# A fused two-block transformer step: TensorE products ordered by tiling, output projections with PSUM tiles taken one by one, and at most four weight pieces waiting for their split

## The chip, the cores and the metric

One NeuronCore of a Trainium2 chip runs the whole program in one launch. The metric is the device time of one execution in microseconds. In the profile PE is TensorE, PEld its weight loads, DVE VectorE, ACT ScalarE, POOL GpSimd and SP SyncE, which issues nearly all DMAs.

## The reference

256 tokens of width 1024 pass through two blocks. All inputs and outputs are float32.

```python
# first block
h = rms_norm(x, norm_mix_g)
(f_q, f_k, f_v, f_f, n_q, k_c, v_c, k_s, v_s, k_w, v_w, n_g, g_a, g_b) = split_cols(h @ w_in)
out_a = fox_attention(...) @ w_fox_up          # 8 heads of 64, with forget gates
out_b = nsa_attention(...) @ w_nsa_up          # compressed, selected and window branches
x = x + (sigmoid(g_a) * out_a + sigmoid(g_b) * out_b) @ w_out
x = x + hierarchical_moe(rms_norm(x, norm_ffn_g), ...)   # 16 experts, 2 per token, SwiGLU of width 512
# second block, two layers
h = rms_norm(x, g_pre)
q_h, f_h, i_h, z_h, q_a, k_a, v_a, z_a = split(h @ w_in)
o_h = rms_norm(hgrn2(q_h, f_h, i_h, lb), g_head) * silu(z_h)     # 8 heads of 128
o_a = sliding_window_attention(rotary(q_a), rotary(k_a), v_a, sinks) * silu(z_a)   # 16 heads of 64
x = x + rms_norm(concat(o_h, o_a) @ w_out, g_post)
```

## The kernel before

**Stages.** The program runs layer 1 of the first block (`layer1`), the experts (`moe`), and two hybrid layers (`hybrid`). Its stages lie in the trace at about 0 to 250 us, 250 to 490 us, 500 to 748 us and 748 to 1003 us. Between two stages an `Edge` adds the result to x, normalises it and transposes it for the next projection.

**A planner writes the order.** The code does not issue instructions directly. Each piece of work is a generator, a task, which yields operations; `Sched.run` (L331) keeps a modelled clock for every engine, and picks for each engine the next operation of all tasks by a key: operations that cannot start within 40 ns of the engine's clock come after those that can, then the smaller priority number goes first, then the older task. Priorities (L409) are P_EDGE -1, P_SPLIT 0, P_EVAC 1, P_SIDE 2, P_LATE 3, P_MAIN 9. The order so found is fixed in each engine's queue when the program is built; on the chip an instruction that isn't ready holds up those behind it on its engine. Waits of a task for another (`wait`, `Flag`) are waits in the planner only: they shape the order. All operations are issued on one line, L216, so the trace tells them apart by tile names. Where the model finds TensorE idle, `keep_warm` (L790) fills in products of a tile of ones (`warm<-ones`).

**Products.** The big projections split both operands into two float32r parts and do three products for each float32 one (`mm3`, `mm3_col`); these use the whole 128 by 128 array. Their outputs go to four PSUM tiles (`acc`); everything else shares four more (`bank`). Other products are plain float32, which the trace shows as two records each. Some use half of the array: 64 output columns (`128*64`: the experts, `bank<-ha` in the scores of hgrn2, `bank<-ap,kv` in the attention's second product), or 64 rows (`64*128`: `bank<-kv,qaT`, the attention's first product), or both. Transposes are products with an identity (`bank<-cp,...`).

**Weights.** `loader` (L512) loads pieces of 1 MB in a fixed plan into 23 shared slots of 1 MB, while fewer than `K.raw_max` are loaded and unused (3 in most of the program, up to 19 in the experts). A piece of a projection is then split: ScalarE writes the high part (`w<-raw`), VectorE the low one (`w<-raw,w`), in two halves, while fewer than `K.half_max` halves are in use. The experts' pieces are used as they are (`"whole"`, `"pair"`). Splits have P_SPLIT, those of output projections P_LATE.

**The experts** (L1342 on). Each expert e takes up to 64 tokens. The main task does gate and up, gu(e): 16 float32 products of 512 columns in pairs that write the two halves of the PSUM partitions (32 records `bank<-raw,xt`); then down(e - 1) (16 records `bank<-raw,route`). Beside them run `rows_of(e)` (L1460: the one-hot rows of the expert by two transposes, and four small products; it writes `ws`, the weights that hidden(e) scales with), `hidden(e)` (L1529: the SwiGLU, then two transposes to hT for down(e)), and `combine(e)` (L1546: down(e)'s result is scaled and added to four `acc` tiles by four products `acc<-rows`). For every four experts `group` gathers tokens by products of x, split by `halves` (L1477) into `xh` and `xl` once.

**The output projection** (`out_proj`, L678) takes all four `acc` tiles first:

```python
    ps = []
    for i in range(4):
        p = yield from acc_tile(K, [128, 512])
        ps.append(p)
```

In a hybrid layer there are four groups of inputs. Groups 0 and 1 are the hgrn2 heads 0 to 3 and 4 to 7, and the main task waits for a group's heads before it goes on to it; groups 2 and 3 are the attention. The last projection is z3: `c_z` (L1802) reads its `acc` tile in four steps on ScalarE and VectorE and only then releases it, and `heads(3)` (L1888) goes on from there to `og`, which group 1 reads.

## Time and profile before

| what | us |
|---|---|
| median of 3 runs (lowest, highest) | 1006.81 (1002.85, 1007.44) |
| the profiled execution | 1005.22 |
| its span, first to last instruction | 1003.4 |
| PE busy in the span | 975.9 |
| DVE busy | 701.4 |
| ACT busy | 496.7 |

A row of the timeline gives start, busy time, engine, line, operation, the tiles out<-in, rows*columns of the array and the moving operand's size, and how many like records follow each other; a bracket gives idle time before it and who ended it. Matmuls are pipelined, and their ends are modelled, so the time that a product takes of the engine is read from start to next start. A PE that is shown as busy may be filling in ones.

### The profile page before, as it was taken

How to read it: one execution, taken by the hardware profiler on the slowest of the kernel's cores; microseconds unless marked ns; L12 is line 12 of the kernel's file. 1: busy time of each engine (PE TensorE's matmuls, PEld its weight loads, DVE VectorE, ACT ScalarE, POOL GpSimd, SP SyncE). 2: the span in 40 equal slices, each digit the busy share in tenths (PEclk: the TensorE clock that was granted, in tenths of full speed). 3: DMA queues.
4: the chain of work that ended last, by engine and by line, in shares of the span. 5: the costliest groups of instructions: out<-in, count | busy, mean ns of one | idle time of the engine just before them, and what ended most of it. 6: DMA issues, size and time to landing. Idle time of an engine off the chain costs nothing.

```text
span 1003.4 us, 16635 instructions
## 1 busy us (share of the span) xinstructions
PE 975.9 (97%) x6335; PEld 748.5 (75%) x6335; DVE 701.4 (70%) x1755; ACT 496.7 (50%) x1054; POOL 23.2 (2%) x64
## 2 busy tenths in 40 slices
PE   7999999999999999999899999999999999999998
PEld 6877898897434343434588979888888897988887
DVE  5777888685364444545656898999768489899942
ACT  5556679741121111114335658668664365866841
POOL 0101000000000000000000000000000000000000
PEclk9999999999999999999999999999999999999999
DMA  8822593797899999989910224433936232442321
GB/s 299 293 81 85 170 318 113 266 378 269 302 390 388 407 409 409 409 343 391 363 63 1 84 84 128 130 104 120 336 122 218 67 103 86 130 146 102 125 107 42
DMA packets 106578, 210.33 MB, mean 210 GB/s; under 512 B 6174, under 2 KB 54544, under 8 KB 106496
## 3 DMA queue, kind: packets, MB, share of 16 engines
q1 hardware_dynamic: 105248, 206.00, 57.3%
q0 software_dynamic: 1248, 3.22, 1.0%
q8 instruction: 52, 0.85, 0.4%
q14 instruction: 30, 0.25, 0.1%
HBM read 208.16 MB, written 1.05 MB: 208 GB/s over the span
## 4 chain that ended last, share of the span: by engine, by line
PE 46%; DVE 8%; ACT 1%; issue 1%; DVEq 0%
PE acc L216 32%; PE bank L216 12%; DVE ha L216 3%; DVE w L216 2%; PE warm L216 1%; DVE ap L216 1%; ACT ha L216 1%; DVE hb L216 1%; DVE hn L216 0%; DVE rows L216 0%; DVE tiny L216 0%; DVE x L216 0%; DVE og L216 0%; DVE za L216 0%; ACT w L216 0%
## 5 line engine op out<-in xcount | busy, mean ns | idle before, releaser
L216 DVE TENSOR_TENSOR w<-raw,w 128x1024 fp32r<-128x1024 f32 (+1 forms) x196 | 233.2, 1211 | 28.5 <-ACT w L216 27.4
L216 PE MATMUL acc<-hh,w 128*128 128x256 f32 x1280 | 247.4, 289 | 0.0
L216 ACT ACTIVATE w<-raw 128x1024 fp32r<-128x1024 f32 (+1 forms) x196 | 198.7, 1040 | 46.7 <-PE acc L216 26.4
L216 PEld LDWEIGHTS acc<-hh,w 128*128 128x128 f32 x1280 | 202.9, 192 | 6.2 <-issue 4.1
L216 PE MATMUL acc<-hl,w 128*128 128x256 f32 x640 | 184.8, 289 | 0.0
L216 PE MATMUL acc<-w,hh 128*128 128x512 f32 (+2 forms) x512 | 155.5, 380 | 0.2
L216 PEld LDWEIGHTS acc<-hl,w 128*128 128x128 f32 x640 | 122.6, 192 | 2.3 <-issue 0.7
L216 PE MATMUL bank<-raw,xt 128*64 128x512 f32 x512 | 118.1, 599 | 1.2 <-DVE xt L216 1.2
L216 PEld LDWEIGHTS acc<-w,hh 128*128 128x128 f32 x512 | 92.6, 188 | 17.3 <-issue 2.2
L216 PE MATMUL acc<-w,hl 128*128 128x512 f32 (+2 forms) x256 | 96.6, 377 | 0.0
L216 PE MATMUL acc<-w,og 128*128 128x512 f32 x384 | 88.7, 390 | 0.0
L216 PEld LDWEIGHTS acc<-w,og 128*128 128x128 f32 x384 | 71.9, 188 | 14.8
L216 ACT ACTIVATE route<-bank,route 128x256 f32<-128x256 f32 x16 | 7.6, 473 | 144.9 <-PE bank L216 144.9
L216 PEld LDWEIGHTS bank<-raw,xt 128*64 128x64 f32 x512 | 33.6, 136 | 58.5 <-issue 53.0
L216 DVE TENSOR_TENSOR ha<-ha 128x128 f32<-128x128 f32 (+5 forms) x216 | 69.3, 352 | 0.6
L216 ACT ACTIVATE ap<-ap,tiny 128x256 f32<-128x256 f32 (+1 forms) x98 | 42.9, 448 | 49.0 <-DVE tiny L216 36.5
L216 PE MATMUL bank<-raw,route 128*64 128x512 f32 x256 | 60.3, 604 | 0.0
L216 PEld LDWEIGHTS acc<-w,hl 128*128 128x128 f32 x256 | 48.3, 189 | 8.2 <-issue 1.0
L216 PE MATMUL warm<-ones 128*128 128x256 f32 x275 | 40.1, 297 | 4.6 <-ACT ones L437 2.4
L216 PEld LDWEIGHTS warm<-ones 128*128 128x128 f32 x275 | 36.3, 198 | 8.1 <-ACT ones L437 2.4
L216 PEld LDWEIGHTS bank<-raw,route 128*64 128x64 f32 x256 | 17.4, 138 | 31.8 <-issue 29.5
L216 PE MATMUL bank<-ha 128*64 128x96 f32 (+2 forms) x608 | 37.9, 246 | 0.0
(276 smaller groups left out, 1330.3 us busy)
## 6 DMA issues: line engine op xcount, KB each, us to landing
raw<-in_w_in_dram SPq DMA_DIRECT2D x68, 1024.0 KB, 7.5
raw<-in_w_gate_dram SPq DMA_DIRECT2D x64, 512.0 KB, 8.9
raw<-in_w_up_dram SPq DMA_DIRECT2D x64, 512.0 KB, 9.9
raw<-in_w_down_dram SPq DMA_DIRECT2D x32, 1024.0 KB, 11.5
raw<-in_w_out_dram SPq DMA_DIRECT2D x20, 1024.0 KB, 5.2
raw<-in_cmp_k_w_dram SPq DMA_DIRECT2D x2, 1024.0 KB, 5.7
raw<-in_cmp_v_w_dram SPq DMA_DIRECT2D x2, 1024.0 KB, 5.8
raw<-in_w_fox_up_dram SPq DMA_DIRECT2D x2, 1024.0 KB, 12.2
```

The lines of the kernel that those rows point to most:

```text
L216: go = lambda: f(*a, **k)
```

## The change

The planner now knows tilings. An operation on TensorE has a mode: whether its rows and its columns are at most 64, for plain float32 products; all others count as whole. Its model adds 95 ns (`SWITCH`) to a product of another mode than the last, and 2 ns in place of 53 for the second of two products side by side. In the choice of the next product, one of a task between P_EDGE and P_MAIN whose mode is not the current one goes behind the main task until 1.5 us (`GATHER`) after it was ready.

In the experts, a flag for each one, `gate[e]`, is set when gu(e) has been issued. `rows_of(e)` does its mask on VectorE as before and then waits for `gate[e]`; the transposes of `hidden(e)` wait for `gate[e + 1]`; the four products of `combine(e)` wait for `gate[e + 2]`. `hidden` and `combine` of the last two experts have P_EDGE. `halves` does its work in 8 pieces of 256 columns in place of 2 of 1024.

`out_proj` takes each of its four PSUM tiles when its first product comes. The loader counts, in `K.parts`, loaded pieces that are to be split, and loads a further one only while there are fewer than four.

```diff
--- before.py
+++ after.py
@@ -82,11 +82,12 @@
 
 class Op:
 
-    __slots__ = ("alts", "ins", "outs", "half", "ready", "banks", "rows")
+    __slots__ = ("alts", "ins", "outs", "half", "ready", "banks", "rows", "mode")
 
     def __init__(self, alts, ins, outs, half=(0, 2)):
         self.alts, self.ins, self.outs, self.half, self.ready = alts, ins, outs, half, None
         self.banks = ()
+        self.mode = None
 
 
 class _Eng:
@@ -140,6 +141,7 @@
         self.cols = [0.0, 0.0]
         self.readers = {}
         self.work, self.cold = [], True
+        self.mode, self.turned = (False, False), False
         self.fill = self.halfway = None
         self.slot = {}
         self.acc = {}
@@ -220,6 +222,7 @@
             half = (h, h + 1)
         o = Op([(eng, op, cost, go)], reg(ins), reg(outs), half)
         if eng == "PE":
+            o.mode = (ins[0].shape[0] <= 64, aps[0].shape[0] <= 64) if op == "matmul" and ins[-1].dtype == F32 else (False, False)
             o.rows = ins[0].shape[0] / 128 * min(1.0, n / 0.6 / cost if op == "matmul" and ins[-1].dtype == F32 else 1.0)
         else:
             o.banks = {self.slot.get(x.tensor.name, x.tensor.name) for x in aps if str(x.space) == "PSUM"}
@@ -271,6 +274,11 @@
     def _product(self, o, start, cost):
         lo, hi = o.half
         start = max(start, self.clk["PE"])
+        if o.mode != self.mode:
+            self.mode = o.mode
+            start += SWITCH
+            self.clk["PE"] = start
+            self.cols = [max(c, start) for c in self.cols]
 
         self.cold = self.activity(start) < (WARM[1] if self.cold else WARM[0])
         if self.cold:
@@ -278,7 +286,7 @@
 
         other = max(o.ready, self.cols[lo]) + cost
         beside = hi - lo == 1 and other <= self.clk["PE"] + 100
-        end = max(start + 53, other) if beside else start + cost
+        end = max(start + 2, other) if beside else start + cost
         if not beside:
             self.work.append((start, end, o.rows))
         for h in range(lo, hi):
@@ -360,7 +368,11 @@
                                     if e != eng:
                                         r = max(r, end + self.LAT[e])
                             late = r > c + (HOLD if t.prio == P_EDGE else 40)
-                            key = (late, r if late else 0.0, -1 if t is self.halfway and eng == "PE" else t.prio, t.seq)
+                            prio = -1 if t is self.halfway and eng == "PE" else t.prio
+
+                            if eng == "PE" and t.pend.mode != self.mode and P_EDGE < t.prio < P_MAIN and r < t.pend.ready + GATHER:
+                                prio = P_MAIN + 0.1
+                            key = (late, r if late else 0.0, prio, t.seq)
                             if pick is None or key < pick[0]:
                                 pick = (key, r, t, alt)
                 if pick is not None and (best is None or pick[1] < best[1]):
@@ -410,6 +422,7 @@
 
 WINDOW, WARM, FILL = 3413.0, (0.43, 0.7), (350.0, 0.7)
 TO_PE, IDLE = 200.0, 150.0
+SWITCH, GATHER = 95.0, 1500.0
 HOLD = 200
 SLOTS = 23
 TINY = 11
@@ -438,6 +451,7 @@
     K.plan, K.next, K.hold = [], 0, 0
     K.accs, K.banks = Res(4), Res(4)
     K.slots, K.tinies = Res(SLOTS), Res(TINY)
+    K.parts = 0
     K.raws, K.raw_max, K.halves, K.half_max = 0, 3, 0, 4
     K.eps = K.const.tile([128, 1], F32, name="eps")
     nc.vector.memset(K.eps, EPS)
@@ -486,6 +500,9 @@
     done = False
 
 
+WHOLE = ("whole", "pair")
+
+
 class Unit:
     def __init__(self, key, pieces, a, n, how):
         self.key, self.pieces, self.a, self.n, self.how = key, pieces, a, n, how
@@ -518,8 +535,10 @@
     def load():
         yield ("if", lambda: K.go)
         for i, u in enumerate(K.plan):
-            yield ("if", lambda: K.raws < K.raw_max and K.slots.free)
+            whole_ = u.how in WHOLE
+            yield ("if", lambda: K.raws < K.raw_max and K.slots.free and (whole_ or K.parts < 4))
             K.raws += 1
+            K.parts += not whole_
             raw, s = yield from big(K, [128, 2048], "raw")
             rv = raw[:, :u.a * u.n].rearrange("p (a n) -> p a n", a=u.a)
             for src, c in u.pieces:
@@ -540,12 +559,13 @@
         u.flag[j].done = True
         if all(f.done for f in u.flag):
             K.raws -= 1
+            K.parts -= 1
             K.slots.release(raws.pop(i)[1])
 
     sch.spawn(load(), P_SPLIT)
     for i, u in enumerate(K.plan):
         yield wait(loaded[i])
-        if u.how in ("whole", "pair"):
+        if u.how in WHOLE:
             u.half = raws.pop(i)
             u.flag[0].done = True
             continue
@@ -679,14 +699,13 @@
 
 
 
-    ps = []
-    for i in range(4):
-        p = yield from acc_tile(K, [128, 512])
-        ps.append(p)
+    ps = {}
     n = len(groups)
     us = {}
 
     def go(g, c, j, t):
+        if 2 * t + c not in ps:
+            ps[2 * t + c] = yield from acc_tile(K, [128, 512])
         oh, ol = groups[g][1]()
         wh, wl = yield from half(K, us[g][c], j)
         for a in range(2):
@@ -1446,6 +1465,8 @@
     t_w = [sp(weights(t), P_EVAC) for t in range(2)]
     groups = {}
 
+    gate = [Flag() for _ in range(NE)]
+
     class Group:
         pass
 
@@ -1459,10 +1480,11 @@
 
     def rows_of(e):
 
-        yield wait(t_w, t_rows.get(e - 1), ys.get(e - 2))
+        yield wait(t_w, t_rows.get(e - 1))
         for t in range(2):
             yield nc.vector.tensor_scalar(dup[:, t].rearrange("p (i s) -> p i s", i=2),
                                           K.c("slot")[:, None, :].to_broadcast([128, 2, CAP]), posm[:, t, e:e + 1], None, op0=OP.is_equal)
+        yield wait(gate[e] if e else None, ys.get(e - 2))
         p2, b_ = yield from bank(K, [128, 258])
         for t in range(2):
             yield nc.tensor.transpose(p2[:, t * 128:(t + 1) * 128], dup[:, t], ident)
@@ -1479,7 +1501,9 @@
         for nm in ("xh", "xl"):
             xhl.append((yield from big(K, [128, 2, D], nm, F32R)))
         for t in range(2):
-            yield from split(K, *(a[0][:, t].rearrange("p (k d) -> p k d", k=8) for a in xhl), K.x[:, t].rearrange("p (d k) -> p k d", k=8))
+            for k in range(0, 8, 2):
+                yield from split(K, *(a[0][:, t].rearrange("p (k d) -> p k d", k=8)[:, k:k + 2] for a in xhl),
+                                 K.x[:, t].rearrange("p (d k) -> p k d", k=8)[:, k:k + 2])
 
     def both(a, b):
         yield wait(a)
@@ -1534,6 +1558,7 @@
         yield nc.vector.scalar_tensor_tensor(s, pg[:, 0], r, s, op0=OP.mult, op1=OP.mult)
         yield nc.vector.scalar_tensor_tensor(s, pg[:, 1], r, s, op0=OP.mult, op1=OP.mult)
         K.banks.release(b_)
+        yield wait(gate[e + 1] if e < NE - 1 else None)
         ph, b_ = yield from bank(K, [128, 2, 128])
         for b in range(2):
             yield nc.tensor.transpose(ph[:, b], s[:, 128 * b:128 * b + 128], ident)
@@ -1552,8 +1577,9 @@
             w = ws[r, 0, e:e + 1]
             yield scaled(K, ty[r, c], py[r], w)
             yield nc.vector.scalar_tensor_tensor(ty[o, c], py[r], w, ty[r, c].bitcast(F32), op0=OP.mult, op1=OP.subtract)
-        yield wait([sp(part(c), P_EVAC if e < NE - 1 else P_EDGE) for c in range(2)])
+        yield wait([sp(part(c), P_EVAC if e < NE - 2 else P_EDGE) for c in range(2)])
         K.banks.release(b_)
+        yield wait(gate[e + 2] if e < NE - 2 else None)
         for t in range(2):
             for c in range(2):
                 yield nc.tensor.matmul(acc[2 * t + c][0], P2[:, e % 2, t], ty[:, c], start=(e == 0), stop=(e == NE - 1))
@@ -1573,7 +1599,7 @@
                     yield nc.tensor.matmul(py[64 * c:64 * c + 64], hT[:, e % 2, b, 64 * h:64 * h + 64], w[:, b, 512 * c:512 * c + 512],
                                            start=(h + b == 0), stop=(h + b == 2))
             drop_whole(K, u)
-        ys[e] = sp(combine(e, py, b_), P_EVAC if e < NE - 1 else P_EDGE)
+        ys[e] = sp(combine(e, py, b_), P_EVAC if e < NE - 2 else P_EDGE)
 
     def bounds():
         K.raw_max -= 1
@@ -1604,11 +1630,12 @@
                     c = w.rearrange("p i (b f) -> p i b f", b=2)[:, :, a, 256 * h:256 * h + 256]
                     yield nc.tensor.matmul(pg[64 * h:64 * h + 64], g.xt[:, k, j], c, start=(k == 0), stop=(k == 7))
             drop_whole(K, u)
+        gate[e].done = True
         if j == 3:
             K.slots.release(g.s_x)
             if q < 3:
                 sp(group(q + 1), P_EVAC)
-        hid[e] = sp(hidden(e, pg, b_), P_EVAC)
+        hid[e] = sp(hidden(e, pg, b_), P_EVAC if e < NE - 2 else P_EDGE)
         if e == 1:
             for i in range(4):
                 a = yield from acc_tile(K, [128, 512])
```

## Rows read from the trace of the kernel before

**Rows 1.** The page: busy us, busy tenths in 40 slices, output projections' products.

```profile
PE 975.9 (97%) x6335; PEld 748.5 (75%) x6335; DVE 701.4 (70%) x1755; ACT 496.7 (50%) x1054; POOL 23.2 (2%) x64
...
DVE  5777888685364444545656898999768489899942
...
L216 PE MATMUL acc<-w,og 128*128 128x512 f32 x384 | 88.7, 390 | 0.0
```

**Rows 2.** Windows: stretch, us, busy PE, PEld, DVE, ACT, POOL, clock, DMA.

```profile
575.00:600.00 25.00, 24.40 (x191) 18.92 (x191) 24.66 (x82) 12.14 (x31) 0.00 (x0) 1.00 0.18 53
```

**Rows 3.** Timeline of TensorE, one expert: start, busy us, operation, shapes, count.

```profile
329.51 3.60 PE L216 MATMUL bank<-raw,route 128*64 128x512 f32 x16
333.05 0.44 PE L216 MATMUL bank<-cp,route 128*128 128x128 f32 x2
333.41 2.79 PE L216 MATMUL bank<-raw,xt 128*64 128x512 f32 x12
336.14 1.21 PE L216 MATMUL acc<-rows 128*128 128x512 f32 x4
337.19 0.38 PE L216 MATMUL bank<-cp,route 128*128 128x128 f32 x2
337.40 0.51 PE L216 MATMUL bank<-route 128*128 128x2 f32 x4
337.84 4.51 PE L216 MATMUL bank<-raw,xt 128*64 128x512 f32 x20
342.18 1.03 PE L216 MATMUL bank<-raw,route 128*64 128x512 f32 x4
```

**Rows 4.** The same view, an excursion to 64 columns in a hybrid layer.

```profile
658.76 0.28 PE L216 MATMUL acc<-hl,w 128*128 128x256 f32 x1
658.88 0.40 PE L216 MATMUL acc<-hh,w 128*128 128x256 f32 x2
659.21 0.68 PE L216 MATMUL bank<-ha 128*64 128x64 f32 x8
659.82 0.39 PE L216 MATMUL acc<-hl,w 128*128 128x256 f32 x1
660.04 0.40 PE L216 MATMUL acc<-hh,w 128*128 128x256 f32 x2
```

**Rows 5.** Timeline of three engines where TensorE stands after expert 3's start.

```profile
291.63 4.04 DVE L216 TENSOR_TENSOR xl<-x,xh 128x1024 fp32r<-128x1024 f32 x2
...
296.00 0.43 PE L216 MATMUL bank<-cp,route 128*128 128x128 f32 x2 [1.46 <-DVE route L216]
```

**Rows 6.** Timeline, the end of the experts' stage.

```profile
467.66 3.60 PE L216 MATMUL bank<-raw,route 128*64 128x512 f32 x16
...
471.36 0.46 ACT L216 ACTIVATE route<-bank,route 128x256 f32<-128x256 f32 x1
...
478.87 0.41 PE L216 MATMUL bank<-cp,route 128*128 128x128 f32 x2 [3.94 <-DVE route L216]
...
479.98 1.98 PE L216 MATMUL bank<-raw,route 128*64 128x512 f32 x4
...
486.31 0.74 DVE L216 TENSOR_SCALAR rows<-bank,route 64x512 fp32r<-64x512 f32 x1 [6.02 <-PE bank L216]
```

**Rows 7.** Groups of instructions, 467.66 to 478.8 us: count, busy us, mean ns.

```profile
L216 DVE TENSOR_TENSOR w<-raw,w 128x1024 fp32r<-128x1024 f32 x8 | 9.4, 1222 | 4.4 <-ACT w L216 4.3
```

**Rows 8.** Windows: 5 us of the same stretch, columns as in rows 2.

```profile
480.00:485.00 5.00, 5.00 (x16) 1.73 (x17) 0.29 (x1) 0.00 (x0) 0.00 (x0) 0.66 1.09 358
```

**Rows 9.** Timeline, last projection to output projection, first hybrid layer.

```profile
696.75 5.18 PE L216 MATMUL warm<-ones 128*128 128x256 f32 x42
...
702.08 0.74 DVE L216 SCALAR_TENSOR_TENSOR hb<-acc,lbt,hb 128x512 f32<-128x512 f32 x1
...
702.99 1.87 PE L216 MATMUL acc<-w,og 128*128 128x512 f32 x7
...
711.78 0.69 DVE L216 TENSOR_TENSOR og<-hb,og 128x512 fp32r<-128x512 f32 x1 [0.70 <-ACT og L216]
```

## The prediction

> **What bounds the kernel now.** I read the page first, for the engine that the span belongs to. PE is busy 97% of it, VectorE 70%, and VectorE's digits stand at 8 and 9 in most slices of the hybrid layers, at 3 to 5 in the experts [rows 1]. So TensorE's stream of products sets the time, with VectorE close behind it in the hybrid layers: in one window of 25 us it is busy 24.66 us, more than PE's 24.40 [rows 2]. Next I read TensorE's order of products in the timeline, stage by stage, for what in that stream isn't useful work. Three things stand out, and the change touches all three.
>
> The first is the price of an interruption by products of another tiling. An undisturbed run of 20 expert records takes 337.84 to 342.18, 4.34 us, so 0.434 us for each pair of products side by side. The 16 records before a change of tiling take 3.54 us against 3.47 at that rate, and the two transposes at 333.05 take 0.36 us to the next start where the same two inside a longer stretch, at 337.19, take 0.21 [rows 3]. One interruption thus costs 0.07 + 0.15 = 0.22 us on top of its own products. In a hybrid layer the last two float32r products before an excursion to 64 columns take 0.33 us against 0.24, and the first after it 0.22 against 0.12 [rows 4]: 0.09 + 0.10 = 0.19 us. Going through TensorE's order I count 20 such excursions in layer 1, 44 in the experts, and 31 in each hybrid layer, 126 in all; at about 0.2 us they hold some 25 us, which is the most that grouping could give back.
>
> The second is two stretches in which TensorE waits. Near expert 3 it stands 1.46 us for a VectorE row mask that is queued behind two pieces of `xl`, 4.04 us long [rows 5]. From the end of gu(15) at 467.66 to the end of down(15) at 486.31 the stage takes 18.65 us, though its products (down(14) from 467.66, then two transposes, four products of combine(14), down(15)) are some 9 us of work. The third is in the hybrid layers: after the last projection TensorE fills in ones from 696.75 until shortly before the output projection's first product at 702.99 [rows 9]; the second hybrid layer repeats it, at 946.11.
>
> **The change part by part.**
>
> (a) Experts, ordered by gates. Before, one expert has two interruptions: the transposes of `hidden`, and `combine` with `rows_of` [rows 3]. After, all of these lie between gu(e) and down(e - 1), one interruption. That saves 0.22 us an expert; over the 14 full ones, 3.1 us. Of the 44 excursions 28 are these; the rest belong to the gathers of four experts, of which I take a quarter to merge, 4 x 0.22 = 0.9 us. Inside the new group float32r follows float32, for which I take back 0.5 us. Sum: -3.5 us; ends 0 and -6. The price is a dependence: down(e - 1) now needs a copy of transposes that were made just before it. The group's own other products cover that: 336.14 to 337.84 is 1.70 us of them [rows 3], and the copy with a hop on either side is below 1 us (the copy of the last expert takes 478.87 to 479.98, transposes included, 1.11 us [rows 6]). If that cover were gone, it would cost up to 1.1 us an expert. `hidden(e)` now starts some 2.5 us later, since `rows_of(e)` gives it its scale; it has a whole expert of 12.7 us (329.51 to 342.18) for it, and so costs nothing. Those gates are the planner's, and nothing new waits on a queue except what the order implies.
>
> (b) `halves` in 8 pieces. The mask no longer queues behind 2 us pieces, and it isn't needed before gu(e) ends. The 1.46 us go: -1.5 us; ends 0 and -2. The added instructions (6 more on each of two engines) lie in slices where VectorE is half idle [rows 1].
>
> (c) The end of the experts. hidden(15) could begin at 467.66, yet its first ScalarE step is at 471.36 and its transposes at 478.87, 11.2 us later [rows 6], because 8 splits of 1.22 us, 9.4 us of VectorE [rows 7], have the higher priority. P_EDGE puts it ahead. New chain: the group after gu(15), 1.70 + 0.36 = 2.1 us, then the copy of `ws`, which is still behind splits (P_SIDE): 0.6 to 3 us, then hidden's five steps, about 3.3 us with hops: 6 to 8.4 us. Then down(15): before, 479.98 to 486.31, 6.3 us, at a mean granted clock of 0.66 of full speed in 480 to 485 [rows 8], so between the two levels of 1.2 and 2.4 GHz, after TensorE had done little since 471.2; at the full clock the same 16 records take 3.54 us [rows 3]. So 11.2 to about 8, and 6.3 to about 4.3, since combine(14) shares the engines: -5 us; ends -1 and -8. What is late next is the edge after combine(15), which the change leaves as it is. The splits that are pushed back have until 500 us.
>
> (d) Hybrid layers, products. A product is held at most 1.5 us for company, and 31 excursions in the 130 us before 697 come 4.2 us apart, so about a third merge: 10 x 0.19 = 1.9 us a layer. Attention products that run together gain a little more, not counted. VectorE is nearly full there, so I take 2.0 us at most as the middle; ends +2 and -5. Layer 1 in the same way: 20 excursions, 7 merged: -1.5 us; ends +1 and -3.
>
> (e) Output projection, tiles one by one. Three of four `acc` tiles are free at 696.75; only z3's is held until c_z's last step ends at 702.82 [rows 9]. Group 0 can start at once: 48 products of 0.231 us (88.7 us for 384 [rows 1]) are 11.1 us. It is tempting to book the whole 6.2 us. But group 1 needs heads(3), whose last step ends at 712.47 [rows 9], 15.7 us after the last projection. Before, group 1 could start at 702.99 + 11.1, with some products of heads(3) between, about 714.5; after, at 712.5. So -2.0 us a layer, and a new wait of 2 to 4 us between the groups; ends 0 and -5 (the chain also gets shorter).
>
> (f) At most four unsplit pieces. It binds only between the experts and the first hybrid layer. There 8 halves and four pieces, eight pieces, replace up to 15. The second hybrid layer never has more than three unsplit, and repeats the first one's order with the same idle. 0 us; ends +3 and -1.
>
> Sum: 3.5 + 1.5 + 5 + 2 x (2 + 2) + 1.5 = 19.5 us. The profiled execution took 1005.2 (span 1003.4 and 1.8 around it); it goes to 985.7. It lies 1.6 us below the median of 1006.8, so on the median: **987.3 us**.
>
> **The rivals.**
>
> *The hybrid layers keep their time.* VectorE, not TensorE, could be what sets them, and the output projection's wait only moves. For: rows 2. Against: even there PE is busy for all but 0.6 us, and in most other slices of these layers VectorE's digit is 8 [rows 1]. Then the 8 us of (d) and (e) are missing: 995. The Trainium skill, "TensorEngine Tiling (Array Packing)", section "PSUM Bottleneck", warns that tiling speeds up TensorE but not the evacuation of PSUM, which may become the bottleneck; by it this rival would hold, and the trace bears it out in that one window, not in the whole stage.
>
> *Little is merged.* The modes follow each other within a task (64 rows, whole, 64 columns), so that a hold finds no company. Then (d) and (a)'s gathers go, the output projection and the experts' end shrink to their lower ends: 1 + 2.6 us, 1003, no change that can be told. A measurement of this kernel tells about 0.5%, 5 us.
>
> *Holding back starves VectorE: slower.* Each of 62 excursions in the hybrid layers may be held up to 1.5 us, with its PSUM bank, one of four. If VectorE, full as it is, loses that time, a layer ends later. It decides when the loss passes 19.5 / 62 = 0.31 us an excursion; at 0.5 us it is 31 - 19.5, so 1018. Against it: c_z and heads(3), whose products use the whole array and are never held, end the chain [rows 9]; the attention's outputs are needed only after group 1.
>
> **How the numbers follow.** Forecast 0.60, 977 to 994; the hybrid layers keep their time 0.22, 991 to 1001; little is merged 0.10, 1002 to 1010; slower 0.08. Faster by over 0.5% (below 1001.8): 0.82; within 0.5%: 0.10; slower: 0.08. The range leaves out the last two, which are 0.18, and reaches down to 975, where the ends of (c) and (e) are added to the sum.
>
> **What the profile would show.** One interruption an expert, and a period of 12.4 to 12.5 us in place of 12.67. No idle at `xl`. hidden(15)'s transposes within 9 us of gu(15)'s end, and a granted clock near 1 through down(15). `acc<-w,og` directly after the last projection, with ones between groups 0 and 1. About 20 excursions a hybrid layer. The forecast is wrong if the hybrid layers take as long as before between their first projection and group 1, or if down(e - 1) waits for its copy.

## The result, and the profile after

The changed kernel takes 982.37 us (median of 4 runs, 979.58 to 984.79) beside 1007.12 us for the kernel before on the same chip: a ratio of 0.9762 (of the means), 95% interval 0.9724 to 0.98. The forecast was 987.3 us, in a range of 975 to 1001. The profiled span went from 1003.4 to 980.6 us, 22.9 us less, where the sum was 19.5. Cut at the same events of TensorE's order in both traces, it divides so (us; gu(e) and down(e) are the products of expert e; a hybrid layer's first cut is the start of its first projection, its second the start of the last `z3` product):

| stage | before | after | difference | forecast |
|---|---|---|---|---|
| start to first gu | 250.31 | 250.49 | +0.2 | -1.5 |
| first gu to down(14) | 217.35 | 214.45 | -2.9 | -5.0 (a, b) |
| down(14) to first projection | 32.50 | 23.22 | -9.3 | -5.0 (c, f) |
| hybrid 0, projections | 196.47 | 194.52 | -2.0 | -2.0 (d) |
| output projection and edge | 51.79 | 49.02 | -2.8 | -2.0 (e) |
| hybrid 1, projections | 197.58 | 194.16 | -3.4 | -2.0 (d) |
| output projection to the end | 57.46 | 54.73 | -2.7 | -2.0 (e) |

The first projections now start between the transposes of the two halves, so their stretch takes 2.0 us longer (43.76 to 45.75 us). Two of the 9.3 us belong there: the experts' end with its edge gave some 7.3, and hybrid 0's projections -3.9. Of the 9.3 us, 4.3 lie between the start of down(14) and the end of down(15) (18.53 to 14.21 us) and 5.0 behind it, in the edge (13.96 to 9.01 us).

The page of the changed kernel (answers to rows 1):

```profile
PE 955.2 (97%) x6252; PEld 738.4 (75%) x6252; DVE 690.7 (70%) x1754; ACT 503.9 (51%) x1063; POOL 31.0 (3%) x68
```

TensorE is still the limit, 20.7 us less busy. GpSimd is one of two engines that are busier, 31.0 us against 23.2; what it does more comes back below.

TensorE's timeline of one expert (answers to rows 3):

```profile
326.90 0.44 PE L218 MATMUL bank<-cp,route 128*128 128x128 f32 x2
327.09 1.18 PE L218 MATMUL acc<-rows 128*128 128x512 f32 x4
328.11 0.38 PE L218 MATMUL bank<-cp,route 128*128 128x128 f32 x2
328.32 0.50 PE L218 MATMUL bank<-route 128*128 128x2 f32 x4
328.76 3.65 PE L218 MATMUL bank<-raw,route 128*64 128x512 f32 x16
332.24 7.04 PE L218 MATMUL bank<-raw,xt 128*64 128x512 f32 x32
339.21 0.44 PE L218 MATMUL bank<-cp,route 128*128 128x128 f32 x2
```

One interruption is left, and down(e - 1) starts with no idle in front of it: the copy is covered. The period is 339.21 - 326.90 = 12.31 us, 0.36 us shorter than before; the forecast said 12.4 to 12.5.

The timeline of three engines near expert 3 (answers to rows 5):

```profile
290.47 4.58 ACT L218 ACTIVATE xh<-x 128x256 fp32r<-128x256 f32 x8
...
291.15 4.55 DVE L218 TENSOR_TENSOR xl<-x,xh 128x256 fp32r<-128x256 f32 x8
...
296.62 0.93 PE L218 MATMUL acc<-rows 128*128 128x512 f32 x3 [0.26 <-ACT route L218]
...
298.36 0.36 PE L218 MATMUL bank<-rows,xh 128*128 128x256 f32 x1 [0.82 <-DVE rows L218]
```

The small pieces still stand in one block, and TensorE still waits after it, 0.26 + 0.82 us in place of 1.46; the second wait is for masks of the gather (`rows`), which VectorE begins at 297.80, behind 1.3 us of small `lbt` steps.

The timeline at the experts' end (answers to rows 6), and a window of 5 us there (answers to rows 8, columns as in rows 2):

```profile
463.08 0.44 PE L218 MATMUL bank<-cp,route 128*128 128x128 f32 x2
...
464.94 3.65 PE L218 MATMUL bank<-raw,route 128*64 128x512 f32 x16
...
467.29 2.36 DVE L218 TENSOR_TENSOR w<-raw,w 128x1024 fp32r<-128x1024 f32 x2 [1.82 <-ACT w L218]
...
469.57 0.15 DVE L218 COPY route<-bank 128x2 f32<-128x2 f32 x1
469.83 0.47 ACT L218 ACTIVATE route<-bank,route 128x256 f32<-128x256 f32 x1
...
473.79 0.44 PE L218 MATMUL bank<-cp,route 128*128 128x128 f32 x2 [0.54 <-DVE route L218]
...
475.56 3.65 PE L218 MATMUL bank<-raw,route 128*64 128x512 f32 x16
...
479.15 2.05 PE L218 MATMUL warm<-ones 128*128 128x256 f32 x15
...
488.16 0.40 PE L218 MATMUL acc<-w,hh 128*128 128x512 f32 x1
```

```profile
475.00:480.00 5.00, 5.00 (x26) 2.10 (x25) 4.97 (x6) 2.51 (x4) 0.00 (x0) 1.00 1.05 384
```

hidden(15) waits for the copy of `ws` at 469.57, which stands behind splits (`w<-raw,w`), as the forecast said. down(15) takes 3.6 us at a granted clock of 1.00, where it took 6.3, 1.6 of them three products of combine(14) in its midst. The first projection follows its end by 9.0 us.

The timeline at the output projection's start (answers to rows 9):

```profile
682.80 5.39 PE L218 MATMUL acc<-w,og 128*128 128x512 f32 x23
...
692.13 2.21 POOL L218 TENSOR_TENSOR sq<-hb,sq 128x512 fp32r<-128x512 f32 x1 [17.70 <-ACT sq L218]
...
694.40 0.50 PE L218 MATMUL bank<-sq,ones 128*128 128x512 f32 x1 [0.52 <-POOL sq L218]
...
696.35 1.59 PE L218 MATMUL warm<-ones 128*128 128x256 f32 x12
...
697.78 3.61 PE L218 MATMUL acc<-w,og 128*128 128x512 f32 x15
```

The output projection follows the last projection at once. Group 0's 48 products are over at 696.35; ones fill 1.4 us, and group 1 starts at 697.78, 15.1 us after the last projection; before, group 0 itself started 6.4 us after it, and group 1 17.9 us. Ahead of that stands something that the forecast had not counted: a step of heads(3) on GpSimd, 2.21 us, for which TensorE stands 0.52 us.

### The profile page after: what moved, and what is told of

The parts are those of the page before. It is cut to its first block, busy times and chain, and to the rows that moved or that the text cites. A ratio compares the mean times of both kernels' runs of the same rounds, so it can differ in the third digit from the quotient of the medians.

```text
span 980.6 us, 16483 instructions
## 1 busy us (share of the span) xinstructions
PE 955.2 (97%) x6252; PEld 738.4 (75%) x6252; DVE 690.7 (70%) x1754; ACT 503.9 (51%) x1063; POOL 31.0 (3%) x68
## 4 chain that ended last, share of the span: by engine, by line
PE 67%; DVE 11%; DMA 10%; issue 6%; ACT 4%; POOL 1%; SPq 1%; DVEq 0%; POOLq 0%; ACTq 0%
PE acc L218 44%; PE bank L218 22%; DMA raw<-in_w_up_dram 6%; DVE w L218 3%; DMA raw<-in_w_down_dram 3%; DVE ha L218 2%; DMA raw<-in_w_in_dram 2%; ACT ap L218 2%; DVE ap L218 1%; DVE hb L218 1%; ACT w L218 1%; POOL sq L218 1%; PE warm L218 1%; DVE rp L218 1%; DVE cb L218 1%
## 5 line engine op out<-in xcount | busy, mean ns | idle before, releaser
L218 DVE TENSOR_TENSOR w<-raw,w 128x1024 fp32r<-128x1024 f32 (+1 forms) x196 | 234.7, 1220 | 22.9 <-ACT w L218 22.5
L218 PE MATMUL bank<-raw,xt 128*64 128x512 f32 x512 | 114.9, 598 | 3.8 <-DMA raw<-in_w_up_dram 2.9
L218 PEld LDWEIGHTS bank<-raw,xt 128*64 128x64 f32 x512 | 36.5, 138 | 73.9 <-issue 64.7
L218 PEld LDWEIGHTS acc<-w,og 128*128 128x128 f32 x384 | 71.6, 188 | 14.7
L218 DVE COPY route<-bank 128x2 f32<-128x2 f32 (+1 forms) x31 | 8.8, 283 | 61.7 <-PE bank L218 61.7
L218 PE MATMUL warm<-ones 128*128 128x256 f32 x192 | 32.2, 313 | 4.3 <-ACT ones L450 2.4
L218 PE MATMUL bank<-ha 128*64 128x96 f32 (+2 forms) x608 | 35.8, 244 | 0.1
```

The lines of the kernel that those rows point to most:

```text
L218: go = lambda: f(*a, **k)
```

## The experiments

All are the changed kernel with one edit, but for the last. Times move by a few us between executions, and most edits by 1 to 8: by the intervals of the ratios only two of the single edits, a1_old_pairs and b1_no_limit, are clear of the changed kernel. So the stages of the profiles, one execution each, are read beside the medians (us, same cuts as above; the median of the kernel before beside them was 1004.74, 1005.84 and 1005.19 in the three sets of four).

| kernel | first gu | down(14) | first proj. | hybrid 0 | edge | hybrid 1 | end | median | ratio to before |
|---|---|---|---|---|---|---|---|---|---|
| changed | 250.49 | 214.45 | 23.22 | 194.52 | 49.02 | 194.16 | 54.73 | 982.37 | 0.9762 |
| a1_four_tiles | 251.57 | 214.86 | 22.84 | 194.52 | 51.62 | 194.15 | 57.36 | 988.48 | 0.9818 |
| a1_no_hold | 248.60 | 216.02 | 24.13 | 197.81 | 48.27 | 197.39 | 54.37 | 988.20 | 0.9814 |
| a1_old_pairs | 249.45 | 224.98 | 24.96 | 196.93 | 48.35 | 196.41 | 54.03 | 996.84 | 0.9916 |
| a1_no_gates | 251.11 | 216.11 | 20.45 | 194.49 | 49.02 | 194.01 | 54.70 | 980.61 | 0.9762 |
| b1_evac | 249.33 | 214.90 | 26.53 | 194.54 | 53.98 | 194.13 | 54.70 | 987.72 | 0.9819 |
| b1_last_free | 251.42 | 217.22 | 18.36 | 194.54 | 49.08 | 193.96 | 54.74 | 980.76 | 0.9759 |
| b1_order | 249.29 | 214.12 | 24.60 | 194.56 | 47.58 | 194.02 | 53.25 | 980.40 | 0.9752 |
| b1_first_free | 247.08 | 213.95 | 22.62 | 194.68 | 49.04 | 194.00 | 56.97 | 981.91 | 0.9765 |
| b1_two_pieces | 250.47 | 216.25 | 21.25 | 194.54 | 54.00 | 193.94 | 58.52 | 986.86 | 0.9810 |
| b1_no_limit | 251.15 | 215.25 | 26.31 | 192.83 | 49.06 | 194.03 | 54.73 | 987.16 | 0.9837 |
| c1_light | 249.98 | 215.51 | 25.01 | 194.60 | 52.68 | 193.93 | 56.97 | 985.74 | 0.9799 |
| c1_best | 247.17 | 219.37 | 18.37 | 194.62 | 46.74 | 193.96 | 52.45 | 975.76 | 0.9709 |

Where the order of a stage is the same, the hybrid columns repeat within 0.2 us and the first column, layer 1, within 2.3 us (249.29 to 251.57). Nine kernels have the same order of products in layer 1, and TensorE stands idle 2.3 to 2.4 us in each shortly before 114 us. In six the granted clock is then 0.66 to 0.70 from 112 to 117 us, in b1_evac, b1_order and b1_two_pieces 1.00; the six take 249.98 to 251.57, the three 249.29 to 250.47. From down(14) to the first projection, four kernels of the same order (changed, b1_first_free, b1_order, b1_two_pieces) take 21.25 to 24.60 us, and from the first gu to the first projection 236.57 to 238.72. The two columns of the output projection have steps of 2 to 5 us between kernels that don't touch them: those are GpSimd's, below.

**a1_four_tiles**: the tiles of the output projection.

```diff
-    ps = {}
+    ps = []
+    for i in range(4):
+        p = yield from acc_tile(K, [128, 512])
+        ps.append(p)
...
-        if 2 * t + c not in ps:
-            ps[2 * t + c] = yield from acc_tile(K, [128, 512])
```

> The changed kernel, but the output projection takes its four PSUM tiles together again. Theory: what the early start gave is bounded by heads(3), which group 1 waits for in any case, so each hybrid layer loses only the 2.8 us that the stretch from the last projection to the next layer's first product had gained: first acc<-w,og about 6 us after the last z3 product instead of at once, no ones between groups 0 and 1, and 2.5 to 3 us more a layer, 5 to 6 us in all, so about 988. Rival 1: the early start was worth its whole 6 us and something else ate the rest: 6 us a layer, 994. Rival 2: the stretch got shorter for another reason (fewer interruptions around it): under 1 us a layer, 982 to 984.

988.48 us (ratio 0.9818, 0.9794 to 0.9842). The two output projections take 2.60 and 2.63 us more, no other column moves beyond its spread, and the first product comes 5.5 us after the last projection. So the early start is worth what heads(3) leaves of it and not its 5.5 us: the theory holds.

**a1_no_hold**: holding products back.

```diff
-SWITCH, GATHER = 95.0, 1500.0
+SWITCH, GATHER = 95.0, -1.0
```

> The changed kernel, but no product is held back for company (the limit of 1500 ns set below zero); the price of 95 ns for a change of tiling stays in the planner's clock. Theory: holding products is what shortened the two hybrid stages before their output projections (by 4.25 and 3.4 us), the stretch of qa1 foremost, so both come back: 7 to 8 us, with 29 to 31 excursions a layer in place of 24, about 990. Rival 1: that gain came from the planner's other model of pairs (2 in place of 53 ns), not from holding: 0 to 2 us, 982 to 985. Rival 2: holding costs VectorE time elsewhere, so that the kernel gets faster without it: 978 to 981.

988.20 us (0.9814, 0.9789 to 0.9838): the hybrid layers take 3.3 and 3.2 us more, the experts 1.6, layer 1 some 2 us less. So without holding the hybrid layers are not shorter than before. But the number of interruptions does not set their time: there are 25 excursions a layer without holding and 24 with it, and with 25 the layer takes as long as before with 31. The windows of the first hybrid layer's projections tell more: first the changed kernel, with the stretch of the `qa1` products below, then the kernel without holding, then the kernel before.

```profile
488.16:682.80 194.64, 192.45 (x1553) 171.78 (x1551) 165.53 (x447) 120.32 (x248) 6.08 (x11) 1.00 0.36 112
565.20:580.36 15.16, 15.16 (x105) 11.52 (x104) 15.16 (x42) 5.78 (x9) 0.00 (x0) 1.00 0.22 71
```

```profile
488.75:686.69 197.94, 193.44 (x1553) 172.37 (x1551) 168.29 (x449) 122.27 (x252) 5.66 (x11) 1.00 0.35 110
566.00:585.28 19.28, 18.51 (x145) 13.85 (x144) 19.21 (x68) 10.22 (x25) 0.00 (x0) 1.00 0.18 55
```

```profile
500.15:696.75 196.60, 194.51 (x1541) 171.79 (x1540) 163.94 (x441) 120.64 (x245) 3.83 (x9) 1.00 0.27 87
```

The 64 products `bank<-kv,qaT` of the attention alone, in the same windows and the same order of kernels (stretch, us, busy PE, clock, DMA):

```profile
488.16:682.80 194.64, 8.55 (x64) 1.00 0.36 112
```

```profile
488.75:686.69 197.94, 9.60 (x64) 1.00 0.35 110
```

```profile
500.15:696.75 196.60, 10.59 (x64) 1.00 0.27 87
```

The products are the same 1553 with and without holding. TensorE is idle 194.64 - 192.45 = 2.2 us with holding and 4.5 us without, and without it its busy time is 1.0 us longer, as much as the `qaT` products lose. In the kernel before it was idle only 196.60 - 194.51 = 2.1 us. So against that kernel holding took no idle time away. What got shorter is TensorE's busy time, by 2.1 us in this layer and 3.6 in the second, and the products in half of the array did that: the same 416 of them take 31.1 us of TensorE before, 29.3 without holding and 27.8 with it (from start to next start, in either layer). Without holding the planner's new prices save the first part of that and lose it again in waits; holding adds the second part and takes the waits away. In the stretch in which VectorE is full (15.16 of 15.16 us) TensorE no longer stands: the attention's products have gone out of it. Without holding TensorE reaches products whose VectorE step isn't done and stands for each, up to 0.9 us. That holding gives those steps time is the reading of these rows; no run shows it alone, and the planner's 95 ns for a change of tiling was not undone alone.

**a1_old_pairs**: the price of a pair in the planner.

```diff
-        end = max(start + 2, other) if beside else start + cost
+        end = max(start + 53, other) if beside else start + cost
```

> The changed kernel, but the planner again counts 53 ns between the starts of two products side by side, in place of 2. Theory: the figure moves only the planner's clock by 0.05 us a pair, and the order changes little: within 2 us of 982. Rival: the shorter qa1 stretch (15.2 in place of 19.9 us) comes from this figure, since with it the planner believed TensorE to be busier than it was: the stretch goes back to 19 to 20 us in both hybrid layers, 989 to 992.

996.84 us (0.9916, 0.99 to 0.9933), the dearest of all, and neither theory had the place. The hybrid layers lose 2.4 and 2.3 us (with 22 excursions a layer, the fewest: the count again does not set the time; the products in half of the array take 28.2 us, and TensorE is idle 4.3 us), but 10.5 us are lost before down(14). TensorE's timeline, then VectorE's:

```profile
463.37 0.44 PE L218 MATMUL bank<-cp,route 128*128 128x128 f32 x2
474.43 4.46 PE L218 MATMUL bank<-raw,route 128*64 128x512 f32 x12 [10.62 <-DVE route L218]
```

```profile
469.41 4.63 DVE L218 TENSOR_TENSOR w<-raw,w 128x1024 fp32r<-128x1024 f32 x4
473.96 0.42 DVE L218 COPY route<-bank 128x256 f32<-128x256 f32 x1
```

Here the cover of the copy that (a) names is gone: hidden(14)'s copy came behind the splits at 473.96, and down(14), queued right behind its transposes, held TensorE's whole queue for 10.6 us. The gates put down(14) right behind those transposes; that the queue is short with the new figure because the planner's clock then agrees better with the chip is the reading, and no run has the old figure without the gates.

**a1_no_gates**: the three waits for `gate` in rows_of, hidden and combine left out.

```diff
-        yield wait(gate[e] if e else None, ys.get(e - 2))
+        yield wait(ys.get(e - 2))
...
-        yield wait(gate[e + 1] if e < NE - 1 else None)
...
-        yield wait(gate[e + 2] if e < NE - 2 else None)
```

> The changed kernel without its three waits for a gate in the experts (transposes, combine and row masks come when their operands are ready, as before). Theory: TensorE's period goes back from 12.31 to 12.6 us an expert, but the weights' stream, which runs at its 409 GB/s from 325 to 425 in either order, sets when the last experts can start: down(14) starts only 1 to 3 us later, and the wait for w_up before gu(13) shrinks from 2.9 us towards 0; 983 to 986. Rival: TensorE sets it alone, and 14 times 0.3 us come back in full: 4 to 5 us, 987.

980.61 us (0.9762, 0.9737 to 0.9787): the gates give nothing as a whole. The period goes back to 12.66 us, so they are worth 0.35 us an expert, more than the 0.22 of (a); gu(15) starts 1.7 us later after the first gu (207.36 against 205.62), yet from the start of down(14) to the first projection it takes 2.8 us less, since hidden(15)'s scale is there when gu(15) ends. My reason for the loss, the weights' stream, doesn't stand (c1_light). The stall of rows 5 goes without any gate. It shows when gu(3) to gu(5), with the halves, is set against gu(7) to gu(9), where no halves are made: 32.00 against 30.18 us in the kernel before (1.82 more), 31.21 against 29.57 in the changed one (1.64), and 29.89 against 29.57 without gates (0.32).

**b1_evac**: the old priorities for the last two experts.

```diff
-        yield wait([sp(part(c), P_EVAC if e < NE - 2 else P_EDGE) for c in range(2)])
+        yield wait([sp(part(c), P_EVAC if e < NE - 1 else P_EDGE) for c in range(2)])
...
-        ys[e] = sp(combine(e, py, b_), P_EVAC if e < NE - 2 else P_EDGE)
+        ys[e] = sp(combine(e, py, b_), P_EVAC if e < NE - 1 else P_EDGE)
...
-        hid[e] = sp(hidden(e, pg, b_), P_EVAC if e < NE - 2 else P_EDGE)
+        hid[e] = sp(hidden(e, pg, b_), P_EVAC)
```

> The changed kernel, but the last two experts keep the old priorities: P_EDGE for combine(15) alone, hidden(14) and hidden(15) behind the splits again; the gates stay. Theory: the priority is what brought hidden(15) forward, so the stretch from the end of gu(15) to the end of down(15), 16.1 us in the changed kernel and 18.4 before, becomes 18 to 21 us, down(15) runs at a lower granted clock, and the kernel takes 3 to 5 us more: 985 to 988. Rival: the gates, which put combine(14) and the transposes next to each other, gave it, and the priority does nothing: within 1 us of 982.

987.72 us (0.9819, 0.9793 to 0.9845). The first projection comes 3.3 us later after down(14), and TensorE's timeline shows hidden(15)'s transposes 14.7 us after gu(15)'s end at 462.37, in place of 10.7:

```profile
462.37 0.44 PE L218 MATMUL bank<-cp,route 128*128 128x128 f32 x2
...
477.11 0.44 PE L218 MATMUL bank<-cp,route 128*128 128x128 f32 x2 [0.24 <-DVE route L218]
```

So the priority brings hidden(15) forward, as (c) said. Its worth is 3.3 us against the changed kernel, and 2.7 to 4.9 us from the first gu to the first projection against the four kernels of one order (241.43 beside 236.57 to 238.72). The profile's other 5 us are GpSimd's.

**b1_last_free**: expert 15's masks and combine(13) without their gate.

```diff
-        yield wait(gate[e] if e else None, ys.get(e - 2))
+        yield wait(gate[e] if 0 < e < NE - 1 else None, ys.get(e - 2))
...
-        yield wait(gate[e + 2] if e < NE - 2 else None)
+        yield wait(gate[e + 2] if e < NE - 3 else None)
```

> The changed kernel, but the row masks of expert 15 and the combination of expert 13 don't wait for the end of gu(15). Theory: hidden(15) takes its scale from those masks, so the gate is what holds down(15) up: the stretch from the end of gu(15) to the end of down(15) falls from 16.1 us to about 11 us, as it did in the kernel without gates (11.1), for one more interruption of 0.2 us: 977 to 979. Rival: without gates the stretch was shorter because gu(15) ended later there and the splits had been done by then, so that here VectorE's splits fill the time: 15 to 16 us, within 1 us of 982.

980.76 us (0.9759, 0.9729 to 0.9789). From the first gu to the first projection 235.58 us in place of 237.67; but c1_best, with the same edit, takes 237.74, so no gain is shown. (c1_best takes 3.2 us more in two stretches in which its granted clock is low: 14.94 against 13.32 from gu(0) to gu(1), and 15.31 against 13.73 from gu(13) to gu(14). From down(14) on both kernels take 18.4 us, where the four of one order take 21.25 to 24.60; but down(14) starts later.) In the timeline TensorE now stands for the copy of hidden(14) in place of hidden(15):

```profile
466.39 0.44 PE L218 MATMUL bank<-cp,route 128*128 128x128 f32 x2
...
468.64 3.65 PE L218 MATMUL bank<-raw,route 128*64 128x512 f32 x16 [1.81 <-ACT route L218]
```

**b1_order**: groups 0, 2, 1, 3.

```diff
-    for u in range(4):
+    for u in (0, 2, 1, 3):
...
-    for g in range(4):
+    for g in (0, 2, 1, 3):
```

> The changed kernel with the hybrid layers' output projection in the order of groups 0, 2, 1, 3, so that a group of attention outputs, done long before, stands between group 0 and the group that needs heads(3). Theory: the wait between the first two groups (ones for 1.4 us and an idle 0.5 us) goes, and heads(3), 16.8 us after the last projection, is covered by 22 us of products: 1.5 to 2.5 us a layer, 977 to 979, no ones inside the output projection. Rival: heads(3) is no longer hurried, and the wait only moves behind the second group or to the next edge: within 1 us of 982.

980.40 us (0.9752, 0.9727 to 0.9777): 1.44 and 1.48 us less in the two output projections, just under the theory's 1.5 to 2.5. The ones and the wait for heads(3) are gone; the 0.53 us for GpSimd stay:

```profile
694.30 0.50 PE L218 MATMUL bank<-sq,ones 128*128 128x512 f32 x1 [0.53 <-POOL sq L218]
694.63 11.75 PE L218 MATMUL acc<-w,og 128*128 128x512 f32 x51
```

**b1_first_free**: nothing is held in layer 1.

```diff
+        self.gather = -1.0
...
-... r < t.pend.ready + GATHER:
+... r < t.pend.ready + self.gather:
...
         K.raw_max = MOE_RAW
+        K.S.gather = GATHER
```

> The changed kernel, but in layer 1 no product is held back for company; from the experts on it is as in the changed kernel. Theory: in layer 1 holding back delays the chain that ends it, since the kernel without any holding reached the first expert 1.9 us earlier (248.60 against 250.49): 1.5 to 2 us faster, about 980.5. Rival: the difference of 1.9 us lay in the start or in the edge before the experts and not in holding: within 0.7 us of 982.

981.91 us (0.9765, 0.9739 to 0.9792), no difference that the timing can tell. In the profiles layer 1 takes 247.08, 247.17 (c1_best) and 248.60 us (a1_no_hold) without holding, and 249.29 to 251.57 in the others: some 2.5 us, which holding costs there. Excursions are 20 without it, as before, and 21 with it.

**b1_two_pieces**: the halves of x in two pieces.

```diff
-            for k in range(0, 8, 2):
-                yield from split(K, *(a[0][:, t].rearrange("p (k d) -> p k d", k=8)[:, k:k + 2] for a in xhl),
-                                 K.x[:, t].rearrange("p (d k) -> p k d", k=8)[:, k:k + 2])
+            yield from split(K, *(a[0][:, t].rearrange("p (k d) -> p k d", k=8) for a in xhl), K.x[:, t].rearrange("p (d k) -> p k d", k=8))
```

> The changed kernel, but the halves of x are made in two pieces of 4 us again, as before. Theory: the mask waits behind a piece again and TensorE stands 1 to 2 us near expert 3, but the weights' stream decides when gu(13) can start, so the wait for weights before gu(13), 2.93 us, shrinks by as much, gu(13) starts 180 to 182 us after the first gu as in the changed kernel (180.9), and the time stays within 1 us of 982. Rival: TensorE's own order decides, and the 1.5 us come back: 984, gu(13) after 182.5 us.

986.86 us (0.981, 0.9789 to 0.9831), but not in its place: gu(4) starts 55.85 us after the first gu (55.78 with small pieces), gu(13) after 181.07, and the first projection 0.2 us earlier after the first gu. From gu(3) to gu(4) it takes 17.78 us in place of 17.55: the pieces are worth 0.2 us. What is longer is both output projections, by 5.0 and 3.8 us, which the edit leaves alone. The timeline of the first, then its windows:

```profile
691.96 4.46 POOL L218 TENSOR_TENSOR sq<-hb,sq 128x512 fp32r<-128x512 f32 x1 [17.70 <-ACT sq L218]
...
696.48 0.80 PE L218 MATMUL bank<-sq,ones 128*128 128x512 f32 x1 [2.76 <-POOL sq L218]
```

```profile
695.00:700.00 5.00, 3.52 (x8) 2.84 (x9) 1.57 (x3) 2.27 (x3) 2.52 (x3) 0.57 1.03 373
700.00:705.00 5.00, 5.00 (x24) 4.53 (x23) 5.00 (x6) 4.85 (x6) 0.00 (x0) 0.75 0.74 284
```

The same GpSimd instruction takes 4.46 us, TensorE stands 2.76 us for it, and its granted clock is at 0.57 and 0.75 in the ten us after. The 4.46 us came in both layers of b1_two_pieces and of c1_light, in the first of b1_evac and in the second of b1_first_free. Where the clock held, in the second layers of c1_light and b1_first_free, the column is 2.24 us longer, as much as TensorE stands longer; in the other four the clock fell and the column is 3.7 to 5.0 us longer. Why that instruction sometimes takes 4.46 us isn't shown.

**b1_no_limit**: no limit of four pieces.

```diff
-            yield ("if", lambda: K.raws < K.raw_max and K.slots.free and (whole_ or K.parts < 4))
+            yield ("if", lambda: K.raws < K.raw_max and K.slots.free)
```

> The changed kernel without the limit of four loaded pieces that wait for their split. Theory: the limit binds only between the experts and the first hybrid layer, where the splits wait for VectorE and not for the load, so nothing changes: within 1 us of 982. Rival 1: the limit keeps SP's queue and slots free, and without it the edge gets 2 to 3 us longer: 985. Rival 2: the limit holds the first projections' weights back: 980.

987.16 us (0.9837, 0.981 to 0.9864). The first projection comes 3.1 us later, hybrid 0 then takes 1.7 us less, 1.4 us in all. But the limit is worth more. TensorE's timeline, from the end of down(15) at 478.64 to the first projection:

```profile
478.64 2.06 PE L218 MATMUL warm<-ones 128*128 128x256 f32 x15
...
491.09 1.06 PE L218 MATMUL bank<-cp,hn 128*128 128x128 f32 x8 [0.53 <-DVE hn L218]
...
492.71 0.39 PE L218 MATMUL acc<-w,hh 128*128 128x512 f32 x1
```

That edge takes 14.06 us, as in the kernel before (13.96), and 8.87 to 9.22 us in every kernel with the limit. Without it all transposes of the second half come ahead of the first projection again. So the limit shortens the edge by 5.0 us, 3.4 net of hybrid 0; why the planner then takes the other order isn't shown. In this execution down(14) to the end of down(15) happened to take 12.25 us in place of 14.21 (12.2 to 15.9 in the kernels whose edit leaves that stretch alone). The timing says still more; its profiled execution was one of its shorter ones.

**c1_light**: less to transfer in the experts. Of `w_down` of experts 4 to 11 only the first 512 columns are loaded and used for both halves, so this kernel leaves out half of those weights and does not compute the reference's result; its products are as many.

```diff
+            n = 512 if 3 < e < 12 else 1024
-            K.plan.append(Unit("d", [(wr[:, 2 * u:2 * u + 2], 0)], 2, 1024, "whole"))
+            K.plan.append(Unit("d", [(wr[:, 2 * u:2 * u + 2, 0:n], 0)], 2, 1024, "whole"))
...
-... w[:, b, 512 * c:512 * c + 512],
+... w[:, b, (n := 512 * c * (not 3 < e < 12)):n + 512],
```

> The changed kernel, but of w_down of the experts 4 to 11 only the first 512 of 1024 columns are loaded and used for both halves: 8.4 MB less to transfer up to gu(13), 20 us at 409 GB/s, with the same products. Theory: the weights' stream is what holds gu(13) up, so the 2.93 us before it go; what then shows is the jump over the overflow's code, 1.8 us before the change, that now lies under it: gu(13) starts 178 to 180 us after the first gu in place of 180.9, and the kernel gains 1 to 3 us, 979.5 to 981.5. Rival: the wait is not the stream but the issue of the transfers or a mask on VectorE that the planner put late: gu(13) after 180.9 us still, within 0.7 us of 982.

985.74 us (0.9799, 0.9772 to 0.9827), and gu(13) starts 180.73 us after the first gu: nothing moved, and my theory falls. The line before gu(13), in the changed kernel and in this one:

```profile
431.42 1.08 PE L218 MATMUL bank<-raw,xt 128*64 128x512 f32 x4 [2.93 <-DMA raw<-in_w_up_dram]
```

```profile
430.71 1.51 PE L218 MATMUL bank<-raw,xt 128*64 128x512 f32 x6 [2.84 <-SPq L1685]
```

The same wait is put down to a transfer in one and to SP's queue in the other. Neither fits: gu(13)'s first `w_up` transfer, the 53rd of 64, was issued at 396.5 us in the changed kernel and landed at 409.3, 22 us before its use. What is there in both is the jump over the overflow's code. The view of that source line, in the changed kernel and in the kernel before:

```profile
L1684 PEldq COMPARE_BRANCH  x1: 6142/6142/6142, 424.9 to 424.9; - x1
```

```profile
L1657 PEldq COMPARE_BRANCH  x1: 6066/6066/6066, 427.0 to 427.0; - x1
```

The jump holds TensorE's queue for 6.1 us in both. Before, it began at 427.00, 0.84 us ahead of the first product of down(11) (427.84), so the products already queued covered all but 1.79 us of it. After, it began at 424.86, just behind the first product of down(11) (424.83), and 2.93 us were left. From gu(12) to gu(13) it costs 16.77 - 13.66 = 3.11 us after (13.66 is the same pair of experts one group earlier) and 14.78 - 12.95 = 1.83 before. No run takes the jump out; that it is the wait rests on these times. And in some executions the clock falls behind it; the windows of c1_best:

```profile
425.00:430.00 5.00, 2.06 (x10) 0.60 (x8) 2.62 (x6) 1.36 (x2) 0.00 (x0) 0.80 1.03 406
430.00:435.00 5.00, 5.00 (x14) 1.47 (x12) 0.00 (x0) 0.00 (x0) 0.00 (x0) 0.52 1.03 406
```

There gu(13) to gu(14) took 15.31 us in place of 12.38.

**c1_best**: the edits of b1_last_free, b1_order and b1_first_free, and heads(3) on VectorE.

```diff
-        yield sch.either(*(e.tensor_tensor(lo, sq, hi.bitcast(F32), op=OP.subtract) for e in (nc.vector, nc.gpsimd)))
+        if hp == 3:
+            yield nc.vector.tensor_tensor(lo, sq, hi.bitcast(F32), op=OP.subtract)
+        else:
+            yield sch.either(*(e.tensor_tensor(lo, sq, hi.bitcast(F32), op=OP.subtract) for e in (nc.vector, nc.gpsimd)))
```

> The changed kernel with four edits together: expert 15's masks and the combination of expert 13 don't wait for gu(15); the hybrid's output projection takes its groups in the order 0, 2, 1, 3; nothing is held back for company in layer 1; and the subtraction in heads(3) stands on VectorE alone (on GpSimd it took 2.2 us, in two profiles 4.46 us, and TensorE waited for it). Theory: the gains add up, 1.6 + 2 + 1 + 1 = 5.6 us: 976 to 978. Rival: they overlap at the edges (an earlier end only moves what the next stage waits for), and the kernel stays at what the better single edits gave: 979.5 to 981.

975.76 us (974.16 to 976.53; ratio 0.9709, 0.9692 to 0.9726), below both kernels. Of the 7.9 us against the changed kernel's profile, 3.3 lie in layer 1, 2.3 in each output projection, and none in the experts' end. (Layer 1's part is as uncertain as that column's spread.) With the subtraction on VectorE, 0.68 us, TensorE doesn't stand for heads(3) at all.

## Why the prediction was right, and which steps were not

The forecast's case came true, 5 us below its middle: the hybrid layers did not keep their time, and holding did not make the kernel slower. "Little is merged" came true in layer 1 alone. That the total is near is in part luck: layer 1 and the experts fell short of their terms by 3.8 us, and the experts' end, the second hybrid layer and the output projections went beyond theirs by 7.2. Two sums of the prediction do not come out: the ends of (c) and (e) lower the forecast by 3 + 6 us to 978.3 and not to 975, and the second rival's 1 + 2.6 us leaves out the 1.5 of (b), with which it stands at 1001.7. The measured time lies inside the range by either. Step by step:

- **(a), (b)**: forecast -5.0, measured -2.9. The period fell by 0.36 us an expert where 0.22 was reckoned, and up to gu(12) that and the merged gathers gave 168.49 - 164.17 = 4.3 us. From gu(12) to gu(13) 2.0 us were lost, 1.3 of them to the jump over the overflow, and the last experts gave 0.6. Some 0.9 us more lie in gu(0) to gu(1), 14.21 us at a low granted clock, where five kernels took 13.32 at a clock of 1.00. At the end the gates hold up hidden(15), so that as a whole they are worth nothing (a1_no_gates). The step that failed is "those gates are the planner's, and nothing new waits on a queue except what the order implies": the order implied a jump that begins later against the products that cover it, a scale for hidden(15) that comes later, and in a1_old_pairs 10.6 us. For expert 15 "it has a whole expert of 12.7 us for it" isn't true; the step counted 16 experts alike. (b) failed too: gu(3) to gu(4) fell from 19.05 to 17.55 us, 1.50 less, but gu(7) to gu(8), without halves, fell by 1.32 as well (17.23 to 15.91). What the halves cost there is 1.82 us before and 1.64 after, so the pieces gave 0.2 and not 1.5; without gates 0.32 is left of it.
- **(c), (f)**: forecast -5 and 0, measured -4.3 up to the end of down(15) and -5.0 behind it, 2.0 of which the first projections give back. The new chain of (c) came as described (`ws` behind splits, the copy, down(15) at full clock); the transposes came 10.7 us after gu(15)'s end and not "within 9". (c)'s size was near, with a spread of 12.2 to 15.9 us in that stretch between executions; the priority gives most of it (b1_evac, 17.4 us, beside 18.5 before). The step that failed is that the edge after combine(15) is left as it is, with (f) at 0: the limit of four pieces took 5.0 us from it (b1_no_limit).
- **(d)**: forecast -2.0 a layer, measured -2.0 (-3.9 without the shift of the first projections) and -3.4. The size was near, the sum not: "about a third merge: 10 x 0.19" expected 20 excursions a layer, and 24 came. The 7 that went are worth 1.3 us at that price, while the products in half of the array took 3.3 us less of TensorE (31.1 to 27.8), which leaves some 2 us a layer for the term that the prediction named and put at nothing, "attention products that run together gain a little more"; no run separates the two. The number of excursions alone did not set the time (31, 25, 24 and 22 excursions: 196.5, 197.8, 194.5 and 196.9 us), since without holding or with the old price of a pair TensorE is idle 4.3 to 4.6 us a layer in front of late steps, in place of 2.1 to 2.3 before and after. The first rival's premise, VectorE full, holds in the `qa1` stretch (15.16 of 15.16 us) and did not keep the layer's time. The Trainium skill, "TensorEngine Tiling (Array Packing)", section "PSUM Bottleneck", had been cited for that rival: it says that the copy out of PSUM may become the bottleneck after a fourfold speedup of TensorE. No run here comes near that, and the trace does not show it for the layer: TensorE's busy time fell by 2.1 us in the first layer and its idle time grew by only 0.1.
- **Layer 1**: forecast -1.5, measured +0.2; holding costs some 2.5 us there. Nothing merged: of 20 excursions 7 were to go, and 21 came. The measured value lies between the term's ends (+1 and -3), but by two effects that cancel: 250.31 us before, 247.1 to 248.6 with the planner's other figures and no holding, 249.3 to 251.6 with it. In the changed kernel the last held products of the compressed attention end at 202.7, ones follow, and the products of `no` start at 203.9 with nothing else left, while without holding (a1_no_hold) 4.9 us of `fo` products still stand there and the `no` products start at 202.0.
- **(e)**: forecast -2.0 a layer, measured -2.8 and -2.7, and 2.6 by undoing it. The reason holds: group 1 waits for heads(3). The new wait was shorter than the 2 to 4 us forecast, 1.4 us of ones; not foreseen was that the planner would send a step of heads(3) to GpSimd.

## What to carry to other kernels

Count an edit of an instruction order by the waits that it moves as well as by the interruptions that it saves: here 25 in place of 31 saved 1.1 us of TensorE's busy time in the first hybrid layer and made 2.4 us of new waits, until products were held back. Measure a gain against the kernel before and not only by undoing the edit: the undone edit showed twice the idle time of the kernel before. When a step is tied to its neighbour in an in-order queue, look for what else is queued behind it: a jump, a scale, a copy behind long VectorE work. Where a planner picks between engines by a fixed price, check the price in the stretch where it matters, and where two groups of work are in either order, put the one that is ready long before between the one that is late and the one it waits for.

## What was not expected of the hardware

One subtraction of 128x512 on GpSimd took 1.28 us in a quiet stretch and 1.89 to 2.22 us inside the output projection, where VectorE was splitting weights, and in six cases 4.46 us; on VectorE it took 0.69. A jump over code that isn't executed held TensorE's queue for 6.1 us, and the idle time behind it was put down to four different things in different traces (TensorE's queue, a transfer, a VectorE step, SP's queue). And an idle time of TensorE of 2.0 to 3.0 us was followed in some executions, not in others of the same order, by 5 to 10 us with a granted clock between 0.5 and 0.9, so that its price was up to twice its length: in layer 1, behind the same 2.3 to 2.4 us, it fell in six kernels of nine. The same 64 attention products took 10.59 us of TensorE in the kernel before and 8.55 us when the planner held them together.
